# A transformer block on one core: the scores of its second attention as three products of high and low parts

## The chip, the core and the metric

The kernel runs on one core of a Trainium2 chip. The core has a matrix engine (TensorE, PE in the profile; its weight loads are PEld), a vector engine (VectorE, DVE), a scalar engine (ScalarE, ACT), a GpSimd engine (POOL) and a queue that starts transfers (SP). Each engine works through its own list of instructions in the order in which they stand there; an instruction waits at the head of its list until the semaphores that it names are set. TensorE adds up in PSUM; the other engines copy from there to SBUF. The metric is the device time of one execution in microseconds (us), and lower is better.

## The reference

Two layers of a block with three branches on 256 tokens `x` and 256 context tokens `ctx`, model width 1024, all in float32. In each layer the normed input goes through one wide projection; from it come a neighbourhood attention (the first attention here), a gated spatial mix, and the attention of this case, an ordinary softmax attention with 8 heads whose queries and keys are 96 wide:

```
s = einsum('bhqd,bhkd->bhqk', q_blk, k) * scale     # 96 wide
p = softmax(s);  out = einsum('bhqk,bhkd->bhqd', p, v)
y = g0 * (y_na @ na_w_o) + g1 * (y_gm @ gm_w_o) + g2 * (y_mla @ mla_w_o)
```

Queries of `x` see 512 keys (context and `x`), queries of the context see its own 256 keys, and the last layer has no queries of the context. The outputs of the three branches are gated, projected and added, and a squared-ReLU MLP follows.

## The kernel before, in words

All activations lie transposed, a feature per partition, and the 512 tokens (256 in what the last layer needs) are the moving columns of the matmuls. Nearly every product is made as three matmuls of high and low parts: a float32 tensor A is split into H, its value rounded to the type `fp32r` (a copy on ACT), and L = A - H (a subtraction on DVE), and the product is H·H + H·L + L·H in one PSUM sum (`mm3`, lines 276 to 278). Weights are loaded by SP and split on the way in (`split1`, lines 115 and 116). The scores of the second attention are the exception: `mla_score` (line 406) multiplies the plain float32 tensors `kml` and `qml` of a head, one matmul for a score tile of 128 queries by 512 or 256 keys.

The stage around the change, in each layer:

- `head_T` (lines 764 to 776) transposes the heads of keys and queries into PSUM (`h_tr`) and scales them into one tile a head: ACT the first 256 columns (line 771), DVE the other 256 where there are four token tiles (line 773).
- `soft_pv` (from line 416) runs four times, once for each pair of heads. For each of its score tiles: the scores `S` (PSUM, two buffers), the negative maximum `nm` on DVE, the exponential `P` on ACT with its sum, the reciprocal `r` and the scaling on DVE, the transposes `pt` on TensorE (PSUM, one buffer), and the copy `PT` of them on ACT. When a pair of heads is through, the products with the values follow (`pvm`), and `split_out` makes the high and low parts `yml` of the pair's output. A pair has four score tiles of 512 keys, and in layer 0 four of 256 keys besides.
- Between these steps TensorE works on the gates (`gate`) and the projections (`z`) of another branch (`merge`, one call of which stands after the attention in the text). `paced` and `tc.issue_after` tie each of their steps to a score matmul, so that these products are spread over the attention as filling work.

The order of the lists is made by a scheduler when the program is built: it takes instructions by priority, as their inputs and buffers come free in its own model of time. Most tiles that outlive a step share one pool of 34 buffers of 128x512 (`g2`, tag `g`): keys, queries, branch outputs, `yml`, and in the second layer the running `x`. A pair of 256-column parts shares one buffer (`parts`).

Of the kernel before, what the change touches and what calls it, by code (L numbers as in the profile page):

```python
# [9 lines left out]
AF = mybir.ActivationFunctionType  # L10
ALU = mybir.AluOpType
# [5 lines left out]
NX = 256  # L17
# [9 lines left out]
def hybrid_block_kernel(tc, a, out):  # L27
    nc = tc.nc
    act = nc.scalar.activation
    vec = nc.vector  # L30
    mm = nc.tensor.matmul

    from contextlib import ExitStack, nullcontext
    with ExitStack() as es:
# [12 lines left out]
        def psum(tag, name):  # L47
            return pp.tile([128, 512], F32, tag=tag, name=name, bufs={"mm": 4, "s": 2, "pt": 1, "pv": 1}[tag])


        def g2(name, dt=F32R):
            return gp.tile([128, 512], dt, tag="g", name=name, bufs=34)

        def views(name, T):

            while True:
                t = g2(name)
                if T == NX:
                    yield t[:, 0:NX]
                    yield t[:, NX:]  # L60
                else:
                    yield t

        def parts(name, T):

            v = views(name, T)
            return next(v), next(v)
# [333 lines left out]

            return score

        def mla_score(K, Q, h):
            def score(s, q0, k0, nk):
                return mm(s, lhsT=Q[h][0:96, q0:q0 + 128], rhs=K[h][0:96, k0:k0 + nk], start=True, stop=True)  # L406

            return score

        def split_out(ps, name, T):  # L410
            H, Lo = parts(name, T)
            act(out=H[:, :T], in_=ps[:, :T], func=AF.Copy)
            vec.tensor_tensor(out=Lo[:, :T], in0=ps[:, :T], in1=H[:, :T], op=ALU.subtract)
            return H, Lo

        def soft_pv(score, V, pv, streams, bias, marks):

            for v in range(streams):
                kts = [0, 1, 2, 3] if v == 0 else [2, 3]
                k0, nk = kts[0] * 128, 128 * len(kts)  # L420
                PT = [gp.tile([128, 4, NX], F32, tag="PT", name="PT", bufs=2) for _ in range(2)]
                for qt in range(2):
                    q0 = v * NX + qt * 128
                    S = []
                    for hh in range(2):
                        s = psum("s", "S")
                        marks.append(score[hh](s[:, :nk], q0, k0, nk).ins)
                        S.append(s)
                    for hh in range(2):
                        s = S[hh]  # L430
                        if bias is not None and v == 0:
                            vec.tensor_tensor(out=s[:, :NX], in0=s[:, :NX], in1=bias[hh][:, qt, :], op=ALU.add)
                        nm = sp.tile([128, 1], F32, tag="nm", name="nm")
                        vec.tensor_reduce(out=nm, in_=s[:, :nk], axis=AX.X, op=ALU.max, negate=True)
                        P = gp.tile([128, 512], F32, tag="P", name="P", bufs=2)
                        sm = sp.tile([128, 1], F32, tag="sm", name="sm")
                        act(out=P[:, :nk], in_=s[:, :nk], func=AF.Exp, bias=nm, accum_out=sm)
                        r = sp.tile([128, 1], F32, tag="r", name="r")
                        vec.reciprocal(r, sm)
                        vec.tensor_scalar(out=P[:, :nk], in0=P[:, :nk], scalar1=r, scalar2=None, op0=ALU.mult)  # L440
                        pt = psum("pt", "pt")
                        for i in range(len(kts)):
                            nc.tensor.transpose(pt[:, i * 128:(i + 1) * 128], P[:, i * 128:(i + 1) * 128], ident)  # L443
                        n = len(kts)
                        turned = act(out=PT[hh][:, :n, qt * 128:(qt + 1) * 128],
                                     in_=pt[:, :nk].rearrange("p (i q) -> p i q", i=n), func=AF.Copy)
                for i, kt in enumerate(kts):
                    for hh in range(2):
                        m = mm(pv[64 * hh:64 * hh + 64, v * NX:(v + 1) * NX], lhsT=V[kt][hh], rhs=PT[hh][:, i, :],
                               start=(i == 0), stop=(i == len(kts) - 1), tile_position=(0, 64 * hh))  # L450
                        if i == 0 and hh == 0:

                            tc.add_manual_dep(m.ins, turned.ins.name, mybir.DependencyInfo(
                                mybir.DependencyClass.Sync, mybir.DependencyReason.DATA), reason="both heads")
# [68 lines left out]
        for l in range(L):  # L523
            last = l == L - 1
# [21 lines left out]
            with tc.issue_after(last_load[0]):  # L546
                if l == 0:
# [8 lines left out]
                                  in_=a["kqrow"][l:l + 1, :].to_broadcast([128, 64]))  # L556
# [4 lines left out]
            for g in range(4):  # L561
                vec.scalar_tensor_tensor(out=bs[:, g, :], in0=rsum[:, g * 128:(g + 1) * 128],
                                         scalar=col[:, 28 + g:29 + g], in1=bs[:, g, :], op0=ALU.mult, op1=ALU.add)
# [74 lines left out]
            for t in range(4):  # L638
                vec.tensor_scalar(out=cnat[t][:, 0:128], in0=cnat[t][:, 0:128], scalar1=rsc[:, t:t + 1], scalar2=None,
                                  op0=ALU.mult)  # L640
# [42 lines left out]
            for t in tts:  # L683
                v = vn[t][:, :512]
                vec.tensor_scalar(out=v, in0=v, scalar1=mv[:, t, 0:1], scalar2=rv[:, t:t + 1], op0=ALU.subtract,
                                  op1=ALU.mult)
# [10 lines left out]
            for g in range(4):  # L697
                ps = psum("s", "sg")
                for t in tts:
                    mm(ps[:, t * 128:(t + 1) * 128], lhsT=vn[t][:, g * 128:(g + 1) * 128], rhs=wsT[:, g, :], start=True,  # L700
                       stop=True)
                y = tmp2("yg")
                for t in tts:
                    vec.scalar_tensor_tensor(out=y[:, t * 128:(t + 1) * 128], in0=ps[:, t * 128:(t + 1) * 128],
                                             scalar=col[:, 24 + g:25 + g], in1=bs[:, g, :], op0=ALU.mult, op1=ALU.add)
                vec.tensor_tensor(out=y[:, :T], in0=y[:, :T], in1=u[g][:, :T], op=ALU.mult)
                H, Lo = parts("yg", T)
# [8 lines left out]
            for j in range(4):  # L716
# [10 lines left out]
                H, Lo = split_out(pv, "yna", T)  # L727
# [10 lines left out]
            for t in range(4):  # L738
# [4 lines left out]
                for hf in range(2):  # L743
                    ps = psum("mm", "kv")
# [3 lines left out]
                        func=AF.Copy)  # L748
# [6 lines left out]
                                  op1=ALU.mult)  # L755
# [4 lines left out]
                                  in1=rb.to_broadcast([128, 8, 32]), op=ALU.mult)  # L760
# [3 lines left out]
            def head_T(tiles, colx, colc, name, n):  # L764
                res = []
                for h in range(8):
                    ps = psum("s", "h_tr")
                    for t in range(n):
                        nc.tensor.transpose(ps[0:96, t * 128:(t + 1) * 128], tiles[t][:, h * 96:(h + 1) * 96], ident)
                    o = g2(name, F32)  # L770
                    act(out=o[0:96, 0:256], in_=ps[0:96, 0:256], func=AF.Copy, scale=colx[0:96])
                    if n > 2:
                        vec.tensor_scalar(out=o[0:96, 256:512], in0=ps[0:96, 256:512], scalar1=colc[0:96], scalar2=None,
                                          op0=ALU.mult)
                    res.append(o)
                return res

            merge(l, 0, ygH, ygL, hH, hL, ymix, T, range(4, 6))
            kmT = head_T(knat, gq[:, 3:4], col[:, 6:7], "kml", 4)

            uq = [split(load(a["uq"][l, k], 768), 384) for k in range(2)]
            qnat = []
            for t in tts:
                ts = slice(t * 128, (t + 1) * 128)
                qn = nat("qnat")
                for hf in range(2):
                    ps = psum("mm", "qm")
# [21 lines left out]
                qnat.append(qn)  # L809
            merge(l, 0, ygH, ygL, hH, hL, ymix, T, range(6, 8))  # L810
            qmT = head_T(qnat, gq[:, 2:3], gq[:, 1:2], "qml", 2 * ns)


            ymH, ymL = [], []
            marks = []
            for j in range(4):
                pv = psum("pv", "pvm")
                soft_pv([mla_score(kmT, qmT, 2 * j + hh) for hh in range(2)],
                        [[vml[t][:, (2 * j + hh) * 64:(2 * j + hh + 1) * 64] for hh in range(2)] for t in range(4)],
                        pv, ns, None, marks)  # L820
                H, Lo = split_out(pv, "yml", T)
                ymH.append(H)
                ymL.append(Lo)
# [35 lines left out]
            if last:  # L859
# [3 lines left out]
                for n in range(KC):  # L863
                    H, Lo = h2[0][n], h2[1][n]
# [3 lines left out]
            for n in range(both, 8):  # L868
                out_chunk(a["wa"][l, 28 + n], n, mixH, mixL, [0], 16, acc)
                if last:  # L870
                    H, Lo = h2[0][n], h2[1][n]
                    act(out=H[:, :NX], in_=xT[n][:, :NX], func=AF.Copy, scale=aa2[:, n:n + 1])
                    vec.scalar_tensor_tensor(out=Lo[:, :NX], in0=xT[n][:, :NX], scalar=aa2[:, n:n + 1], in1=H[:, :NX],
                                             op0=ALU.mult, op1=ALU.subtract)
# [165 lines left out]
```

## Time and profile before

| what | value |
|---|---|
| median of 3 runs | 1408.24 us (1403.92 to 1413.73) |
| profiled execution, its own time | 1407.51 us |
| its span (first to last instruction) | 1405.5 us |
| mean granted TensorE clock | 0.998 |
| TensorE busy | 1372.3 us, 98% of the span |
| VectorE, ScalarE busy | 957.5 us (68%), 703.7 us (50%) |

The profile is of one execution. The busy time of TensorE counts each matmul from its start to the modelled end of its pipeline, so that matmuls that follow each other overlap; how long TensorE is kept by one is read from the start of one to the start of the next. A float32 matmul shows as two records, an `fp32r` matmul as one. The second attention runs from about 331 to 420 us in layer 0 and from about 1107 to 1160 us in layer 1.

### The profile page before, as it was taken

To read this page: it belongs to the slowest core of one execution; us is meant where nothing else is said; L and a number is where in the kernel's file an instruction comes from. 1 tells how busy PE (TensorE), PEld (TensorE's weight loads), DVE (VectorE), ACT (ScalarE), POOL (GpSimd) and SP (SyncE) were. 2 spreads that over 40 slices of the span, in tenths; PEclk is the share of its full clock that TensorE was granted. 3 is DMA by queue.
4 is the path that set the end of the run, shared out by engine and by line. 5 is a ranking of instruction groups with operands and counts; after the bars stand their busy time and mean duration, and the time that the engine had idled before them with its cause. 6 is when DMAs were issued, how large, how long until landed. Compare 5 with 4: busy or idle time off the path is not lost.

```text
span 1405.5 us, 22569 instructions
## 1 busy us (share of the span) xinstructions
PE 1372.3 (98%) x8438; PEld 1160.2 (83%) x8438; DVE 957.5 (68%) x2075; ACT 703.7 (50%) x1440; POOL 58.4 (4%) x35
## 2 busy tenths in 40 slices
PE   5999999999999999999999999999999999999999
PEld 3888767777667789987788888988878879999998
DVE  5666477664563458998766665787777766777775
ACT  4466256543453346623324234566666665656654
POOL 0110000110000000000000000011003000000000
PEclk9999999999999999999999999999999999999999
DMA  9423542234313465665555553442533425655564
GB/s 326 158 80 105 190 140 91 82 95 131 106 52 119 135 191 170 202 201 171 198 198 180 192 183 91 150 137 94 180 106 110 126 80 163 191 179 178 184 182 148
DMA packets 67213, 210.61 MB, mean 150 GB/s; under 512 B 8608, under 2 KB 9632, under 8 KB 67104
## 3 DMA queue, kind: packets, MB, share of 16 engines
q1 hardware_dynamic: 67104, 209.18, 46.2%
q8 instruction: 66, 1.08, 0.3%
q14 instruction: 43, 0.35, 0.1%
HBM read 208.10 MB, written 1.05 MB: 149 GB/s over the span
## 4 chain that ended last, share of the span: by engine, by line
PE 94%; DVE 2%; DMA 2%; ACT 1%; issue 0%; SPq 0%; POOL 0%; ACTq 0%; DVEq 0%
PE o_ps L277 8%; PE o_ps L278 8%; PE o_ps L276 8%; PE f L276 6%; PE f L277 6%; PE f L278 6%; PE gate L276 5%; PE gate L278 5%; PE gate L277 5%; PE b_ps L276 4%; PE b_ps L278 4%; PE b_ps L277 4%; PE pt L443 3%; PE S L406 2%; PE z L276 2%; PE z L277 2%
## 5 line engine op out<-in xcount | busy, mean ns | idle before, releaser
L115 ACT ACTIVATE wh<-raw 128x512 fp32r<-128x512 f32 (+2 forms) x570 | 352.8, 626 | 522.9 <-PE o_ps L277 188.5
L116 DVE TENSOR_TENSOR wl<-raw,wh 128x512 fp32r<-128x512 f32 (+2 forms) x570 | 384.8, 682 | 184.3 <-ACT wh L115 179.6
L276 PE MATMUL f<-hH,wh 128*128 128x258 f32 (+2 forms) x560 | 180.7, 324 | 0.5 <-ACT wh L115 0.5
L278 PE MATMUL f<-hH,wl 128*128 128x258 f32 (+2 forms) x560 | 180.7, 323 | 0.1
L277 PE MATMUL f<-hL,wh 128*128 128x258 f32 (+2 forms) x560 | 180.6, 324 | 0.2 <-DVE hL L266 0.2
L277 PE MATMUL o_ps<-aL,wh 128*128 128x256 f32 (+1 forms) x544 | 176.3, 327 | 1.6 <-DVE aL L909 1.6
L276 PE MATMUL o_ps<-aH,wh 128*128 128x256 f32 (+1 forms) x544 | 175.8, 328 | 0.0
L278 PE MATMUL o_ps<-aH,wl 128*128 128x256 f32 (+1 forms) x544 | 175.5, 327 | 0.0
L276 PE MATMUL gate<-hH,wh 128*128 128x512 f32 (+1 forms) x384 | 140.4, 366 | 0.0
L278 PE MATMUL gate<-hH,wl 128*128 128x512 f32 (+1 forms) x384 | 130.9, 341 | 0.0
L277 PE MATMUL gate<-hL,wh 128*128 128x512 f32 (+1 forms) x384 | 130.4, 340 | 0.0
L276 PEld LDWEIGHTS f<-hH,wh 128*128 128x128 f32 x560 | 105.9, 190 | 10.2 <-ACT wh L115 2.0
L278 PEld LDWEIGHTS f<-hH,wl 128*128 128x128 f32 x560 | 106.1, 190 | 8.5 <-DVE wl L116 0.3
L277 PEld LDWEIGHTS f<-hL,wh 128*128 128x128 f32 x560 | 105.9, 190 | 8.7 <-issue 0.4
L277 PEld LDWEIGHTS o_ps<-aL,wh 128*128 128x128 f32 x544 | 103.0, 190 | 10.6 <-DVE aL L909 2.1
L276 PEld LDWEIGHTS o_ps<-aH,wh 128*128 128x128 f32 x544 | 102.5, 190 | 10.1 <-ACT wh L115 1.2
L278 PEld LDWEIGHTS o_ps<-aH,wl 128*128 128x128 f32 x544 | 102.7, 190 | 8.8
L277 PE MATMUL b_ps<-wl,hH 128*128 128x512 f32 (+2 forms) x288 | 108.3, 379 | 0.0
L278 PE MATMUL b_ps<-wh,hL 128*128 128x512 f32 (+2 forms) x288 | 106.2, 380 | 0.0
L197 DVE SCALAR_TENSOR_TENSOR macc<-rawx,sS,macc 128x512 f32<-128x512 f32 x112 | 78.9, 748 | 39.8 <-DMA rawx<-in_wmod_dram 39.7
L276 PE MATMUL b_ps<-wh,hH 128*128 128x512 f32 (+2 forms) x288 | 103.1, 384 | 0.2 <-ACT hH L265 0.2
L276 PEld LDWEIGHTS gate<-hH,wh 128*128 128x128 f32 x384 | 73.0, 190 | 15.8 <-issue 7.5
(226 smaller groups left out, 2481.6 us busy)
## 6 DMA issues: line engine op xcount, KB each, us to landing
raw<-in_wa_dram SPq DMA_DIRECT2D x147, 512.0 KB, 3.6
raw<-in_w_dram SPq DMA_DIRECT2D x68, 512.0 KB, 3.6
raw<-in_wb_dram SPq DMA_DIRECT2D x32, 512.0 KB, 3.3
raw<-in_wmod_dram SPq DMA_DIRECT2D x32, 512.0 KB, 3.4
rawx<-in_wmod_dram SPq DMA_DIRECT2D x32, 512.0 KB, 4.6
raw<-in_wo_dram SPq DMA_DIRECT2D x24, 512.0 KB, 3.6
rawm<-in_wmod_dram SPq DMA_DIRECT2D x32, 256.0 KB, 6.0
rawx<-in_wmod_dram SPq DMA_DIRECT2D x32, 256.0 KB, 4.3
```

What stands on the lines that cost most here:

```text
L115: act(out=wh[:, :width], in_=src, func=AF.Copy)
L116: vec.tensor_tensor(out=wl[:, :width], in0=src, in1=wh[:, :width], op=ALU.subtract)
L197: vec.scalar_tensor_tensor(out=o, in0=src, scalar=s, in1=o, op0=ALU.mult, op1=ALU.add)
L276: mm(ps, lhsT=sh, rhs=mh, start=first, stop=False)
L277: mm(ps, lhsT=sh, rhs=ml, start=False, stop=False)
L278: mm(ps, lhsT=sl, rhs=mh, start=False, stop=last)
L406: return mm(s, lhsT=Q[h][0:96, q0:q0 + 128], rhs=K[h][0:96, k0:k0 + nk], start=True, stop=True)
L443: nc.tensor.transpose(pt[:, i * 128:(i + 1) * 128], P[:, i * 128:(i + 1) * 128], ident)
```

## The change: three products for each score, and parts made pair by pair

```diff
-        def mla_score(K, Q, h):
+        def mla_score(K, Q):
+            (KH, KL), (QH, QL) = K, Q
             def score(s, q0, k0, nk):
-                return mm(s, lhsT=Q[h][0:96, q0:q0 + 128], rhs=K[h][0:96, k0:k0 + nk], start=True, stop=True)
+                qs, ks = slice(q0, q0 + 128), slice(k0, k0 + nk)
+                mm(s, lhsT=QH[0:96, qs], rhs=KH[0:96, ks], start=True, stop=False)
+                mm(s, lhsT=QH[0:96, qs], rhs=KL[0:96, ks], start=False, stop=False)
+                return mm(s, lhsT=QL[0:96, qs], rhs=KH[0:96, ks], start=False, stop=True)
             return score
+        def split_head(t):
+            H, Lo = g2("hdH"), g2("hdL")
+            act(out=H[0:96, :], in_=t[0:96, :], func=AF.Copy)
+            vec.tensor_tensor(out=Lo[0:96, :], in0=t[0:96, :], in1=H[0:96, :], op=ALU.subtract)
+            return H, Lo
...
+                    if n == 2:
+                        H, Lo = parts(name, NX)
+                        act(out=H[0:96, :], in_=ps[0:96, 0:NX], func=AF.Copy, scale=colx[0:96])
+                        vec.scalar_tensor_tensor(out=Lo[0:96, :], in0=ps[0:96, 0:NX], scalar=colx[0:96], in1=H[0:96, :],
+                                                 op0=ALU.mult, op1=ALU.subtract)
+                        res.append((H, Lo))
+                        continue
...
-                soft_pv([mla_score(kmT, qmT, 2 * j + hh) for hh in range(2)],
+                heads = [[split_head(kmT[h]), qmT[h] if last else split_head(qmT[h])] for h in (2 * j, 2 * j + 1)]
+                soft_pv([mla_score(*z) for z in heads],
```

Each score becomes three `fp32r` matmuls. The keys of all heads, and the queries in layer 0, are still made as float32 tiles by `head_T`; just before a pair's `soft_pv` `split_head` makes `hdH` (ACT) and `hdL` (DVE), 96x512, for its two heads. In layer 1 the queries (256 columns) are split as they leave PSUM.

The change moves instructions at the seam from one pair of heads to the next. On TensorE in layer 0, from the last score tile of the second pair to the first of the third (`S` are scores, `pt` the transposes, `pvm` the products with the values, `gate` the filling work), before:

```order
L449 MATMUL pvm<-PT,vml 64x256 x8
L443 MATMUL pt<-ident,P 128x128 x2
L406 MATMUL S<-kml,qml 128x256
L276 MATMUL gate<-hH,wh 128x512
L277 MATMUL gate<-hL,wh 128x512
L278 MATMUL gate<-hH,wl 128x512
L443 MATMUL pt<-ident,P 128x128 x2
L406 MATMUL S<-kml,qml 128x512
L276 MATMUL gate<-hH,wh 128x512
L277 MATMUL gate<-hL,wh 128x512
L278 MATMUL gate<-hH,wl 128x512
```

and the same place after the change:

```order
L411 MATMUL S<-hdL,hdH 128x256
L412 MATMUL S<-hdH,hdL 128x256
L276 MATMUL gate<-hH,wh 128x512
L277 MATMUL gate<-hL,wh 128x512
L278 MATMUL gate<-hH,wl 128x512
L455 MATMUL pt<-ident,P 128x128 x6
L461 MATMUL pvm<-PT,vml 64x256 x4
L410 MATMUL S<-hdH 128x512
L411 MATMUL S<-hdL,hdH 128x512
L412 MATMUL S<-hdH,hdL 128x512
L276 MATMUL gate<-hH,wh 128x512
```

Before, the first score of the next pair stood between two transposes of the old pair, with filling work around it; now all transposes and value products of the old pair stand in a row, and the next pair's scores behind them. The other two seams of layer 0 read alike (the first has four `mod_ps` matmuls of 256 columns more ahead of the transposes).

On ACT at the same seam after the change (`yml` is the output of the old pair, `hdH` the high parts of the next):

```order
L457 ACTIVATE PT<-pt 128x2x128 x2
L424 ACTIVATE yml<-pvm 128x512
L418 ACTIVATE hdH<-kml 96x512
L418 ACTIVATE hdH<-qml 96x512
L418 ACTIVATE hdH<-kml 96x512
L418 ACTIVATE hdH<-qml 96x512
L449 ACTIVATE P,sm<-S,nm 128x512
```

The four high parts stand behind `yml`, and `yml` waits for `pvm`; DVE has the same order (the low part of `yml`, four `hdL`, then `nm`). In layer 1 the seams read so on TensorE after the change, three times:

```order
L276 MATMUL gate<-hH,wh 128x256
L277 MATMUL gate<-hL,wh 128x256
L278 MATMUL gate<-hH,wl 128x256
L455 MATMUL pt<-ident,P 128x128 x12
L461 MATMUL pvm<-PT,vml 64x256 x8
L410 MATMUL S<-hdH,qml 128x512 x2
L411 MATMUL S<-hdL,qml 128x512
L412 MATMUL S<-hdH,qml 128x512
L276 MATMUL gate<-hH,wh 128x256
```

(at the third seam with `z` in place of `gate`). Before, each group of four transposes there was followed by a score of the next pair and about twelve filling matmuls.

## Rows read from the trace of the kernel before

**Rows 1.** The page, busy time, share of the span and instructions of each engine.

```profile
PE 1372.3 (98%) x8438; PEld 1160.2 (83%) x8438; DVE 957.5 (68%) x2075; ACT 703.7 (50%) x1440; POOL 58.4 (4%) x35
```

**Rows 2.** Stretches of both second attentions: length, busy PE, PEld, DVE, ACT, POOL, clock, DMA.

```profile
330.00:420.00 90.00, 90.00 (x472) 62.60 (x471) 51.95 (x119) 45.75 (x112) 0.00 (x0) 1.00 0.28 88
1107.00:1160.00 53.00, 52.80 (x360) 42.01 (x360) 35.32 (x78) 32.73 (x74) 0.00 (x0) 1.00 0.27 85
```

**Rows 3.** Groups by shape on PE: records, busy us, mean ns; idle before.

```profile
L406 PE MATMUL S<-kml,qml 96*128 96x512 f32 x64 | 32.7, 594 | 0.2 <-ACT qml L771 0.2
...
L406 PE MATMUL S<-kml,qml 96*128 96x256 f32 x32 | 9.7, 383 | 0.0
```

**Rows 4.** Timeline of PE, layer 0, two 512-key scores: start, us, instruction.

```profile
330.98 1.88 PE L406 MATMUL S<-kml,qml 96*128 96x512 f32 x4
332.30 0.80 PE L278 MATMUL gate<-hH,wl 128*128 128x512 f32 x1
332.94 0.40 PE L276 MATMUL gate<-hH,wh 128*128 128x512 f32 x1
```

**Rows 5.** Timeline of PE, layer 0, one 256-key score.

```profile
353.61 0.60 PE L406 MATMUL S<-kml,qml 96*128 96x256 f32 x2
...
354.28 0.39 PE L277 MATMUL gate<-hL,wh 128*128 128x512 f32 x1
```

**Rows 6.** Timeline of PE, first attention of layer 1: two fp32r products and gates.

```profile
1013.43 0.40 PE L399 MATMUL S<-naK,naQ 128*128 128x512 f32 x1
...
1013.90 0.28 PE L276 MATMUL gate<-hH,wh 128*128 128x256 f32 x1
1014.01 0.27 PE L277 MATMUL gate<-hL,wh 128*128 128x256 f32 x1
```

**Rows 7.** Groups by shape on ACT and DVE that split high and low parts.

```profile
L115 ACT ACTIVATE wh<-raw 128x512 fp32r<-128x512 f32 x546 | 340.1, 630 | 502.1 <-PE o_ps L277 188.5 <-PE f L277 118.6 <-DMA raw<-in_wa_dram 72.4
...
L116 DVE TENSOR_TENSOR wl<-raw,wh 128x512 fp32r<-128x512 f32 x546 | 371.3, 687 | 178.1 <-ACT wh L115 173.7 <-PE pt L443 0.2
...
L390 DVE SCALAR_TENSOR_TENSOR naQL<-tr_ps,gq,naQ 64x256 fp32r<-64x256 f32 x16 | 7.7, 483 | 2.3 <-ACT naQ L388 2.0
```

**Rows 8.** Timelines of PE, ACT and DVE, layer 0, around a seam.

```profile
357.38 0.44 PE L443 MATMUL pt<-ident,P 128*128 128x128 f32 x2
357.92 0.39 ACT L445 ACTIVATE PT<-pt 128x256 f32<-128x256 f32 x1 [0.46 <-PE pt L443]
...
367.02 1.08 PE L449 MATMUL pvm<-PT,vml 128*64 128x256 f32 x8
368.15 0.60 ACT L412 ACTIVATE yml<-pvm 128x512 fp32r<-128x512 f32 x1 [0.82 <-PE pvm L449]
368.78 0.69 DVE L413 TENSOR_TENSOR yml<-pvm,yml 128x512 fp32r<-128x512 f32 x1 [1.16 <-ACT yml L412]
```

**Rows 9.** Timelines of layer 1: transposes in a row, and a pair's value products.

```profile
1058.63 0.63 PE L443 MATMUL pt<-ident,P 128*128 128x128 f32 x4 [0.19 <-DVE P L440]
...
1059.30 0.60 ACT L445 ACTIVATE PT<-pt 128x512 f32<-128x512 f32 x1 [0.83 <-PE pt L443]
1059.95 0.66 PE L443 MATMUL pt<-ident,P 128*128 128x128 f32 x4 [0.69 <-ACT PT L445]
...
1151.01 1.95 PE L449 MATMUL pvm<-PT,vml 128*64 128x256 f32 x16
...
1153.00 0.39 ACT L412 ACTIVATE yml<-pvm 128x256 fp32r<-128x256 f32 x1 [2.13 <-PE pvm L449]
```

**Rows 10.** Timeline of PE, layer 1, the first scores of the second attention.

```profile
1106.49 0.79 PE L769 MATMUL h_tr<-ident,qnat 128*96 128x128 f32 x4 [0.20 <-ACT qml L771]
1107.47 1.13 PE L406 MATMUL S<-kml,qml 96*128 96x512 f32 x2 [0.20 <-ACT qml L771]
```

**Rows 11.** Stretches of layer 1, first attention; columns as in rows 2.

```profile
1015.00:1018.40 3.40, 1.84 (x11) 1.21 (x10) 2.33 (x7) 2.73 (x6) 0.00 (x0) 1.00 0.54 154
1018.40:1022.00 3.60, 3.58 (x16) 3.39 (x16) 3.17 (x9) 1.78 (x4) 0.00 (x0) 0.53 0.13 35
1057.00:1061.30 4.30, 2.30 (x13) 1.33 (x13) 2.13 (x7) 2.66 (x6) 0.00 (x0) 1.00 0.30 95
```

## The prediction

> **What bounds the kernel now.** I read the page first: TensorE is busy 98% of the span [rows 1], so a microsecond taken from its list, or put on it, moves the end one for one, and work of another engine counts only where TensorE waits for it. Then the stretches of the changed stage [rows 2]: in layer 0 TensorE is busy all 90 of 90 us, in layer 1 for 52.8 of 53, at the full clock, while VectorE has 58 to 67% and ScalarE 51 to 62%. So there is room beside TensorE for more work of those two, and no slack on TensorE. Last the timelines, for what one score costs TensorE and for how long the steps of a softmax follow each other [rows 4 to 6, 8, 9]. The profiled execution took 1407.51 us, 2.0 more than its span and 0.7 less than the median of the runs; the sums below stand on it.
>
> **The change part by part.**
>
> *Scores.* There are 32 score tiles of 512 keys and 16 of 256: 64 and 32 records [rows 3], two for each. Two 512-key scores start at 330.98, one gate matmul follows, the next begins at 332.94 [rows 4]; less 0.23 for that gate, 1.73 us for two, 0.865 each. For 256 keys: 0.67 us from 353.61 to 354.28 with one gate between, so 0.44 [rows 5]. An `fp32r` product of 512 columns keeps TensorE for 0.235 us (two from 1013.43 to 1013.90), one of 256 for about 0.115 [rows 6]. Three of them are 0.70 and 0.35. Saved: 32 x 0.165 + 16 x 0.09 = **6.7 us**. Those products have 128 rows and the new ones 96; I take no difference for that, and rival 4 is the far end of it.
>
> *Parts.* 24 `hdH` at 0.63 us on ScalarE and 24 `hdL` at 0.69 on VectorE [rows 7], 15.1 and 16.5 us, and 8 new subtractions of 0.48 for the queries of layer 1 (row L390 is the nearest, out of PSUM, 256 columns). Against the idle time of both engines [rows 2] this is covered in the middle of a pair. What it costs if the cover is gone is the next two terms: where TensorE has nothing else in front of it.
>
> *The seams of layer 0, three.* After the change the six transposes, four value products and the first scores of the next pair stand in a row on TensorE, with no filling work between, and TensorE cannot go past a waiting one. I count from the start of the transposes. There is one `pt` buffer, so each of the three pairs of transposes waits until ScalarE has copied the one before: 0.54 us from `pt` to `PT` and 0.39 of copying [rows 8], with the hand-over 0.97, three times 2.9. From `pvm` to ScalarE's `yml` 1.13, from there to VectorE's `yml` 0.63 [rows 8]. The parts of the next pair stand behind these in both lists: on VectorE the rest of `yml`, `hdL` of the keys and `hdL` of the queries, three of 0.69, until the third product can start, and 0.23 for it. Sum 7.0 us. Of this TensorE works 0.8 (transposes, 0.44 each less the 0.17 by which a record is longer than its step), 0.9 (value products) and 0.7 (three products): 2.4. Lost **4.6 us**, three times 13.7.
>
> *The seams of layer 1, three.* Twelve transposes, eight value products, then scores. A turn of four transposes takes 1.32 us where they stand in a row [rows 9], three 4.0. From `pvm` to `yml` 1.99 [rows 9], 0.39 for it, 0.63 for `hdH`, 0.69 for `hdL`, 0.47 for the last two products: 8.1 us. TensorE works 1.4, 1.8 and 0.9 (four products) in it. Lost **4.0 us**, three times 12.0.
>
> *The start of layer 1.* Transposed queries leave PSUM through two buffers. Now each is free only after VectorE's subtraction behind ScalarE's copy: 0.48 and a hand-over of 0.05 more in each of the last three rounds, 1.6. Before, the first score came 0.98 us after the last transposes began [rows 10]; now `hdH` and `hdL` (0.63 + 0.69) stand between, of which two products fill 0.4: 0.9. Together **2.5 us**. In layer 0, 22 matmuls of 512 columns (`z` and `gate`) stand in TensorE's list between the last transposed queries and the first score, 22 x 0.235 = 5.2 us, and VectorE's four parts take 4 x 0.69 = 2.8: nothing.
>
> *The clock.* In the first attention of layer 1 TensorE was busy 1.84 of 3.4 us, with a wait of over a microsecond at the end, and the granted clock then stood at 0.53 for 3.6 us (half speed, 1.2 GHz, for nearly all of it) while TensorE was fully busy; the loss is 3.6 x 0.47 = 1.7 us [rows 11]. Further on it was busy 2.30 of 4.3 us, in a row of transposes as at the seams, and kept the full 2.4 GHz. So the trace has it both ways. At a seam of layer 0 TensorE works 2.4 of 7.0 us, with some 3 us in front of the last two products that hold one product; that is sparser than the stretch that fell, and I take a fall there, 3 x 1.7 = **5.1 us**. A seam of layer 1 works 4.1 of 8.1, more than the stretch that held; I take none. The Trainium skill (TensorE: Matmul & The Clock Gate, HAM oscillation) says that a TensorE left waiting between bursts is throttled to half rate and pays in the next burst, each time anew. By the rule alone every seam and the start would pay, 11.9 us in place of 5.1; rows 11 agree once and disagree once.
>
> Sum: 1407.5 - 6.7 + 13.7 + 12.0 + 2.5 + 5.1 = **1434 us**.
>
> *Bounds.* A seam cannot cost less than the turns alone, if the parts were ready when the value products end: two waits for `PT` between transposes and one before `pvm`, 0.69 each in layer 1 [rows 9] (the second wait stands in its row), about as much in layer 0: 2.1 us. With the start and no fall that gives 1407.5 - 6.7 + 12.6 + 2.5 = 1416. Upward, one exponential (some 0.7 us) or one weight split (0.63 and 0.69) may stand in front of a copy at each seam: six times 0.7, 4 us, on top of the case with every fall.
>
> **The rivals.**
>
> 1. *The clock falls everywhere* (the rule above, Trainium skill): six seams and the start at 1.7 us. 1407.5 - 6.7 + 28.2 + 11.9 = 1441. For it: the wait of half a microsecond or more before the scores at every seam. Against it: the stretch that held.
> 2. *The seams cost only their turns*, 1416, within the measurement's noise of 1% about 1408. For it: `hdH` waits for nothing but its place behind `yml`, and VectorE and ScalarE may have run ahead. Against it: `yml` itself waits for `pvm`, and both lists have the parts behind it.
> 3. *Not slower: the seams cost nothing*, because the old pair's `P` and `PT` are there long before TensorE comes to them, as before, where in 330 to 420 us it never waited [rows 2]. Then the cheaper scores are left: 1407.5 - 6.7 + 2.5 = 1403. It decides at (6.7 - 2.5) / 6 = 0.7 us lost per seam: under that the change is faster. Against it: one `PT` turn alone is 0.97 us with 0.27 of work in it.
> 4. *The scores do not get cheaper*: if each product took the two records of a float32 one, 32 x 1.73 + 16 x 0.88 = 69 us more. The first attention multiplies the same type at one record, so I give it under 1%.
>
> **How the numbers follow.** Chances: the forecast 0.60, rival 1 0.20, rival 2 0.14, rival 3 0.05, rival 4 under 0.01. Predicted 1434. The range leaves out rival 3, most of what lies under the bound of rival 2 and the far end of rival 1: 1416 to 1446; the forecast's own range is 1426 to 1441. A change under 1%, 14 us, cannot be told from none by a few runs of this kernel. Slower by over 1% (from 1422 up) are the forecast and rival 1: 0.81; within 1% are rivals 2 and 3 but for a sliver: 0.17; faster by over 1% would need 14 us, twice all that the scores can save: 0.02.
>
> **What would show it.** In the new profile: scores at one record each, three per tile, about 0.235 us from start to start at 512 keys; at six places a row of `pt`, `pvm`, `S` without filling work, 7 to 8 us long, in which TensorE waits for `PT`, then for `hdH` and `hdL`, 4 to 5 us a place; waits for the queries' VectorE subtraction before the first scores of layer 1; the granted clock at half after the seams of layer 0 and full after those of layer 1. Outside the two stages the lists are the same, so all of the difference must lie in them. It would be wrong if TensorE shows no waits at the seams (rival 3), if it waits for `PT` but not for the parts (rival 2), or if the clock falls after all seams or none.

## The result and the profile after

The changed kernel takes 1439.66 us (median of 4 runs, 1436.75 to 1442.93) where the kernel before took 1410.01 on the same chip: a ratio of 1.0224, 95% interval 1.0202 to 1.0246. Forecast were 1434 us and a range of 1416 to 1446. The profiled execution took 1440.59 us with a span of 1438.6, 33.1 longer than that of before.

The page's busy line of the changed kernel, to be read against [rows 1]:

```profile
PE 1384.7 (96%) x8486; PEld 1174.5 (82%) x8486; DVE 977.3 (68%) x2107; ACT 716.9 (50%) x1464; POOL 59.3 (4%) x35
```

VectorE and ScalarE got 20 and 13 us of work more, which is what the parts cost there, and their share did not rise. TensorE fell from 98 to 96%. Its busy time rose by 12 us although the scores are cheaper: time at half clock counts as busy. So both losses have to be looked for on TensorE, waiting and clock. Its waits in the changed kernel (what waited, for whom: us in total, times, longest):

```profile
PE S L410 <- ACT hdH L418: 9.2, 7, 1.7
PE pt L455 <- ACT PT L457: 6.6, 10, 0.7
PE pt L455 <- DVE P L452: 5.4, 8, 0.9
PE pvm L461 <- ACT PT L457: 3.5, 6, 0.7
PE h_tr L781 <- DVE qml L785: 2.6, 2, 2.0
```

Seven waits of scores for the parts are the six seams and the start of layer 1; six waits of `pvm` for `PT` are the six seams again. One seam of layer 0, as the timeline of three engines shows it (start, us, instruction, idle time before it and who ended that):

```profile
361.70 0.44 PE L455 MATMUL pt<-ident,P 128*128 128x128 f32 x2
362.24 0.38 ACT L457 ACTIVATE PT<-pt 128x256 f32<-128x256 f32 x1 [1.16 <-PE pt L455]
...
362.67 0.44 PE L455 MATMUL pt<-ident,P 128*128 128x128 f32 x2 [0.53 <-ACT PT L457]
...
363.88 0.41 PE L455 MATMUL pt<-ident,P 128*128 128x128 f32 x2 [0.77 <-DVE P L452]
...
364.76 1.40 PE L461 MATMUL pvm<-PT,vml 128*64 128x256 f32 x8 [0.47 <-ACT PT L457]
366.20 0.60 ACT L424 ACTIVATE yml<-pvm 128x512 fp32r<-128x512 f32 x1 [1.50 <-PE pvm L461]
366.69 0.62 ACT L418 ACTIVATE hdH<-kml 96x512 fp32r<-96x512 f32 x1
366.83 0.69 DVE L425 TENSOR_TENSOR yml<-pvm,yml 128x512 fp32r<-128x512 f32 x1 [3.10 <-ACT yml L424]
...
367.44 0.68 DVE L419 TENSOR_TENSOR hdL<-kml,hdH 96x512 fp32r<-96x512 f32 x1
...
367.88 0.79 PE L410 MATMUL S<-hdH 96*128 96x512 f32 x1 [1.72 <-ACT hdH L418]
368.04 0.68 DVE L419 TENSOR_TENSOR hdL<-qml,hdH 96x512 fp32r<-96x512 f32 x1
...
368.90 0.67 PE L412 MATMUL S<-hdH,hdL 96*128 96x512 f32 x1
...
369.37 0.63 PE L276 MATMUL gate<-hH,wh 128*128 128x512 f32 x1
```

Read it down: TensorE turns `pt` and waits for its copy; then `pvm`; then ScalarE's `yml`, which needs `pvm`, and only behind it the first `hdH` of the next pair; on VectorE the same with `hdL`. ScalarE was idle for 1.50 us and VectorE for 3.10 in front of `yml`: they had time for the parts, and the parts stood in the wrong place. The row is 7.67 us from the first `pt` to the first `gate` (forecast 7.0), and the gate matmuls behind it take 0.63 instead of 0.40: the clock is at half.

A score of 512 keys after the change, at full clock, on TensorE's timeline, where [rows 4] show two records of a float32 score:

```profile
374.14 0.40 PE L410 MATMUL S<-hdH 96*128 96x512 f32 x1
374.37 0.40 PE L411 MATMUL S<-hdL,hdH 96*128 96x512 f32 x1
374.60 0.39 PE L412 MATMUL S<-hdH,hdL 96*128 96x512 f32 x1
374.83 0.39 PE L276 MATMUL gate<-hH,wh 128*128 128x512 f32 x1
```

Three products from 374.14 to 374.83 are 0.69 us for 0.865, as in the sum.

What each place cost can be read from stretches of 16 us around the seven rows: three seams of layer 0, the start of layer 1, its three seams (columns as in [rows 2]: length, busy PE, ..., granted clock).

```profile
361.00:377.00 16.00, 12.51 (x56) 8.53 (x56) 8.67 (x18) 7.65 (x19) 0.00 (x0) 0.79 0.22 66
387.00:403.00 16.00, 12.50 (x56) 8.53 (x53) 7.72 (x18) 7.79 (x19) 0.00 (x0) 0.79 0.11 34
416.00:432.00 16.00, 12.51 (x52) 9.01 (x51) 9.17 (x21) 7.28 (x19) 0.00 (x0) 0.79 0.06 22
1115.00:1131.00 16.00, 12.28 (x73) 10.11 (x73) 11.20 (x24) 8.31 (x19) 0.00 (x0) 0.79 0.34 109
1134.00:1150.00 16.00, 12.72 (x81) 9.71 (x80) 8.27 (x18) 7.97 (x18) 0.00 (x0) 0.89 0.12 33
1150.00:1166.00 16.00, 12.65 (x90) 10.35 (x89) 9.61 (x22) 8.96 (x21) 0.00 (x0) 1.00 0.30 92
1168.00:1184.00 16.00, 12.65 (x78) 9.42 (x77) 8.12 (x18) 7.94 (x19) 0.00 (x0) 0.89 0.20 66
```

The loss of a stretch is its idle time plus busy time x (1 - clock). A seam of layer 0: 3.49 + 12.51 x 0.21 = 6.1, three 18.4. The start of layer 1: 3.72 + 2.58 = 6.3, of which 0.9 was idle in the kernel before as well (1097 to 1170 us: 72.08 busy of 73). Its seams: 4.7, 3.4 and 4.7, together 12.8. So 18.4 + 5.4 + 12.8 = 36.6, less 6.7 for the scores is 29.9. The stretches are from the two profiled executions, and these differ by 33.1, so 3.2 us lie in no stretch, and what they are is not shown. That the medians differ by 29.65, close to the 29.9, is luck: the profile of before lies 2.5 under its median, that of the change 0.9 above.

A second way to cut the time, used for the experiments: the stage of layer 0 from the first transpose of its queries to the first output product (`o_ps` from `mix`), and that of layer 1 from the start of the last `z` of its gated branch to the start of the last such output product. Each kernel's times are from its own profiled execution, the ratio is to the kernel before on the same chip.

| kernel | layer 0, us | layer 1, us | ratio (95%) |
|---|---|---|---|
| before | 192.8 | 126.9 | 1 |
| the change | 208.3 | 144.7 | 1.0224 (1.0202 to 1.0246) |
| bare products, no parts | 188.9 | 124.2 | 0.9942 (0.9925 to 0.9959) |
| layer 0 alone changed | 208.6 | 128.4 | 1.0117 (1.0097 to 1.0137) |
| layer 1 alone changed | 192.8 | 143.8 | 1.0128 (1.0108 to 1.0149) |
| parts a pair ahead | 189.9 | 131.7 | 1.0016 (1.0002 to 1.0029) |
| only more buffers | 197.4 | 136.4 | 1.0078 (1.0055 to 1.0101) |
| parts made, not read | 194.3 | 134.5 | 1.0061 (1.0038 to 1.0083) |
| ahead, queries copied | 189.8 | 129.3 | 0.9987 (0.9974 to 0.9999) |
| seams filled | 205.1 | 144.6 | 1.0205 (1.0177 to 1.0233) |
| ahead, first pair float32 | 189.8 | 126.9 | 0.9949 (0.9932 to 0.9966) |
| the change, queries copied | 208.6 | 144.2 | 1.0219 (1.0193 to 1.0244) |

### The profile page after: what moved, and what is told of

Read it like the earlier page. It is cut to its first block, busy times and chain, and to the rows that moved or that the text cites. A ratio compares the mean times of both kernels' runs of the same rounds, so it can differ in the third digit from the quotient of the medians.

```text
span 1438.6 us, 22735 instructions
## 1 busy us (share of the span) xinstructions
PE 1384.7 (96%) x8486; PEld 1174.5 (82%) x8486; DVE 977.3 (68%) x2107; ACT 716.9 (50%) x1464; POOL 59.3 (4%) x35
## 5 line engine op out<-in xcount | busy, mean ns | idle before, releaser
L115 ACT ACTIVATE wh<-raw 128x512 fp32r<-128x512 f32 (+2 forms) x570 | 352.9, 626 | 526.5 <-PE o_ps L277 189.8
L276 PE MATMUL gate<-hH,wh 128*128 128x512 f32 (+1 forms) x384 | 132.5, 345 | 0.0
L859 DVE SCALAR_TENSOR_TENSOR xT<-o_ps,modT,xT 128x256 f32<-128x256 f32 x120 | 54.7, 481 | 44.0 <-PE o_ps L278 43.6
```

Of the source, the lines that this page charges most:

```text
L115: act(out=wh[:, :width], in_=src, func=AF.Copy)
L276: mm(ps, lhsT=sh, rhs=mh, start=first, stop=False)
L859: vec.scalar_tensor_tensor(out=xT[n][:, s], in0=ps[:, p0:p0 + NX], scalar=modT[:, v, mod0 + n:mod0 + n + 1], in1=xT[n][:, s], op0=ALU.mult ...
```

## The experiments

**1. Bare products.**

```
-                    if n == 2:
+                    if False:
...
-                    o = g2(name, F32)
+                    o = g2(name)
...
-                heads = [[split_head(kmT[h]), ...] for h in (2 * j, 2 * j + 1)]
+                heads = [[(kmT[h], kmT[h]), (qmT[h], qmT[h])] for h in (2 * j, 2 * j + 1)]
```

> Three fp32r products per score, no parts: keys and queries are written once as fp32r, the same high part stands in for the low parts (the low parts are left out of the computation). Theory (the scores themselves are cheaper, the seams cost): TensorE keeps its filling work between the transposes and the products at all six seams, no waits for parts, 32 x 0.165 + 16 x 0.09 = 6.7 us less than before, some 1403. Rival (three products are not cheaper than one float32 product): within 2 us of before, or slower.

Measured 1397.45 us against 1405.87, 8.4 less. In the stages the scores bring 3.9 in layer 0 and 2.7 in layer 1: 6.6, where the forecast had 6.7. The rest lies outside the two stages. A part of it can be the half-clock stretch of [rows 11], worth 1.7: the granted clock of this profiled execution is 1.000 over the whole of it. For the medians this is not shown. Between 330 and 430 us TensorE never waits:

```profile
330.00:430.00 100.00, 100.00 (x583) 74.71 (x582) 57.99 (x132) 49.20 (x122) 0.00 (x0) 1.00 0.29 93
```

The saving is real and as large as forecast, and three products in place of one disturb nothing: no wait and no fall of the clock came with them here. What the change loses comes from getting the parts to them: against this kernel it loses 19.4 us in layer 0 (forecast 13.7 + 5.1 = 18.8) and 20.5 in layer 1 (forecast 12.0 + 2.5 = 14.5).

**2 and 3. One layer alone.** In the other layer, the scores stay one float32 product (`mla_score1` is the `mla_score` of before). The edit for layer 0 alone; layer 1 alone has the two cases the other way round:

```
+  heads = [[kmT[h], qmT[h]] for h in ...] if last else [[split_head(kmT[h]), split_head(qmT[h])] for h in ...]
...
+  soft_pv([(mla_score1 if last else mla_score)(*z) for z in heads], ...)
...
-                    if n == 2:
+                    if False:
```

> The change in layer 0 alone, layer 1 as before. By the trace of the changed kernel the stage of layer 0 grew by 15.5 us (forecast 14.7): 1425. If the change of layer 0 also moves the clock of what follows, the time comes out beside this by the 1.7 us of each fall more or less. Rival (the cost goes by the amount of added work on ScalarE and VectorE, evenly): half of 30, 1425 as well, but then without waits of TensorE at the three seams.

> The change in layer 1 alone, layer 0 as before. By the trace of the changed kernel the stage of layer 1 grew by 17.8 us: 1428. By the forecast's terms (4.0 a seam, 2.5 for the start, no fall of the clock) 11.9: 1422. If the clock at the seams falls by chance of phase, other seams than the first and third should show it now, since everything arrives at another time.

Measured 1422.32 and 1424.58 against 1405.87: 16.5 and 18.7. The stages grew by 15.8 and 16.9 where in the whole change they grew by 15.5 and 17.8, so in the stages the two layers' costs add up (the medians' 16.5 and 18.7 add to 35.2, beside 29.65 in the whole change and 33.1 between its profiled executions; the intervals of the ratios leave room for that). With layer 0 alone changed, scores wait three times for `hdH`, 5.2 us in all, which its rival excluded. Layer 1 alone lies between the 1422 of the forecast's terms and the 1428 by the trace. Two sizes are worth a look. With layer 0 alone changed, the untouched layer 1 is 1.5 longer than before: its start, which waited 0.9 us before and held the full clock, waits 1.1 and has a fall of the clock (granted 0.89 over 1116 to 1132 us). And with layer 1 alone changed, the clock did not fall at other seams than in the whole change, which I had expected from chance: the value products show it, 3.35 us long at the first seam, 1.95 at the second, 3.57 at the third.

**4. Parts a pair ahead.** The parts of the next pair are asked for in front of a pair's softmax, in eight more buffers under two tags (`nat`, `bias`) that are idle in this stage.

```
+            heads = pair_heads(0)
             for j in range(4):
                 pv = psum("pv", "pvm")
-                heads = [[split_head(kmT[h]), ...] for h in (2 * j, 2 * j + 1)]
+                nxt = pair_heads(j + 1) if j < 3 else None
                 soft_pv(...)
+                heads = nxt
```

Here `pair_heads(j)` makes the parts of pair `j` by the `split_head` of the change, in the buffers that `head_room` of experiment 5 hands out.

> All the changed arithmetic, but the parts of a pair of heads are made a pair ahead, into eight more buffers (two tags that are idle in this stage). TensorE's list has its filling work at all six seams again. Theory (the seams are the price): six seams and their falls of the clock go, the cheaper scores stay, and the start of layer 1 with its slow release of two PSUM buffers stays at 2.5 to 6: 1406 to 1410, against 1440 of the change. Rival (the price is the parts' work, 24 x 0.63 on ScalarE and 24 x 0.69 on VectorE, crowding the softmax): no more than a few us better than the change, 1430 to 1440, with TensorE waiting for P and PT all over the stages.

Measured 1408.06 us, ratio 1.0016, as the theory had it: the same arithmetic, the same parts, and some 30 us less than the change. TensorE's list has its filling work at all six seams, and neither a wait nor a fall is left there; the start of layer 1 is left (stretches as above):

```profile
330.00:430.00 100.00, 100.00 (x574) 74.33 (x570) 64.03 (x144) 53.61 (x130) 0.00 (x0) 1.00 0.28 90
1094.00:1118.00 24.00, 20.06 (x119) 17.08 (x118) 18.30 (x39) 13.50 (x31) 0.00 (x0) 0.79 0.33 108
1118.00:1170.00 52.00, 52.00 (x405) 46.79 (x403) 34.46 (x75) 32.05 (x71) 0.00 (x0) 1.00 0.29 92
```

VectorE is busy for 64% of those 100 us and ScalarE for 54%, where they had 58 and 51 before [rows 2], and TensorE never waits for them. The stage of layer 1 is 7.5 us above that of the bare products, nearly all of it in the start: 3.9 idle, 1.1 of which the bare products have too, and 20.06 x 0.21 = 4.2 by the clock. The 7.5 are three times the 2.5 that the forecast gave the start.

**5. Only more buffers.** The same eight buffers, but each pair's parts are asked for where the change has them, behind the pair before.

```
+  room = head_room(4 if last else 8)      # so many of tag "g", then 6 of "nat" and 2 of "bias", in turn
...
-            H, Lo = g2("hdH"), g2("hdL")
+            H, Lo = next(room), next(room)
```

> The change with eight more buffers for the parts and nothing else altered: the program still makes the parts of a pair after the pair before. TensorE's list then keeps its filling work at four of the six seams; the second seam of layer 0 and the third of layer 1 stay a row of pt, pvm, S. Theory (too few buffers put the parts behind yml, and each row costs): one row of layer 0 (5.2) and one of layer 1 (4 to 6) above the kernel with parts made a pair ahead, 1417 to 1420 at 1406 of before. Rival (the price is the parts' work or the program's order of parts and pairs): near the change, 1435.

Measured 1416.76 against 1406.78, a ratio of 1.0078. Four of the six seams close by the buffers alone: with more room the scheduler puts those parts forward by itself. The two that stay open (the second of layer 0, the third of layer 1) are rows of `pt`, `pvm` and `S` as in the change. The one of layer 0:

```profile
381.59 0.44 PE L464 MATMUL pt<-ident,P 128*128 128x128 f32 x2 [1.02 <-ACT PT L466]
...
382.79 0.41 PE L464 MATMUL pt<-ident,P 128*128 128x128 f32 x2 [0.76 <-DVE P L461]
...
383.67 1.08 PE L470 MATMUL pvm<-PT,vml 128*64 128x256 f32 x8 [0.47 <-ACT PT L466]
...
386.49 0.79 PE L410 MATMUL S<-hdg 96*128 96x512 f32 x1 [1.73 <-ACT hdg L427]
```

They cost 7.5 and 4.7 us of their stages against the kernel of experiment 4. So at four seams it was the pool of 34 buffers that put the parts behind `yml`: with eight more they moved. The other two close only where the parts are also asked for a pair ahead (experiment 4). Asking a pair ahead without the eight buffers was not run.

**6. Parts made, but not read.** `split_head` runs as in the change, and the scores are one float32 product of `kmT` and `qmT` (the queries of layer 1 are copied as before besides).

```
                 heads = [[split_head(kmT[h]), ...] for h in (2 * j, 2 * j + 1)]
+                heads = [[kmT[h], qmT[h]] for h in (2 * j, 2 * j + 1)]
...
-                soft_pv([mla_score(*z) for z in heads],
+                soft_pv([mla_score1(*z) for z in heads],
```

> All parts made as in the change (and the queries of layer 1 also copied as before), but the scores are one float32 product of keys and queries as before, so nobody reads the parts. Theory (waiting for the parts is the price, making them is not): no waits for hdH or PT at the seams, within 5 us of before, 1406 to 1411. Rival (the work on ScalarE and VectorE is the price): 1420 to 1435.

Measured 1414.76 against 1406.78, 8.0 more: more than the theory's 5, less than the rival's 13 and above, so neither range holds it. The stretches tell where (columns as above):

```profile
330.00:430.00 100.00, 99.31 (x523) 68.85 (x522) 60.69 (x140) 53.74 (x132) 0.00 (x0) 1.00 0.27 90
1096.00:1122.00 26.00, 20.68 (x125) 16.42 (x124) 17.64 (x40) 15.71 (x37) 0.00 (x0) 0.80 0.35 117
1122.00:1180.00 58.00, 57.87 (x418) 47.64 (x417) 39.16 (x86) 37.26 (x83) 0.00 (x0) 1.00 0.27 82
```

Away from the start TensorE waits 0.7 us in layer 0, whose whole stage is 1.5 longer than before, and 0.1 in layer 1; at the start of layer 1 the parts' work comes with 5.3 us of idle time and 4.1 by the clock. There TensorE has few other products left and its transposes wait for ScalarE's copies (4.6 us of waits of `h_tr` for `qml`), and here work put between those copies showed.

**7. The start, mended in part.** As 4, but the queries of layer 1 leave PSUM by one copy of ScalarE, as before, and are split from SBUF (into the same eight buffers and, in layer 1, eight of tag `g` in place of four).

```
-                    if n == 2:
+                    if False:
...
-  qmT[h] if last else split_head(qmT[h], room)
+  split_head(qmT[h], room, T)
```

> Parts made a pair ahead, and the queries of layer 1 leave PSUM as before, by one copy of ScalarE, and are split from there like the keys. Theory: the waits for the VectorE subtraction of the queries (2.6), the wait of the first score (1.4) and the half clock from 1104 to 1114 (5 us) that the kernel with parts a pair ahead shows at the start of layer 1 all go: 9 less, some 1398 to 1400, faster than before by 6 to 8. Rival (those waits only move to the new splits behind the copies): 1403 to 1408.

Measured 1404.60 against 1406.78, ratio 0.9987 (0.9974 to 0.9999): inside the rival's range, though a part of the theory holds. The start, and the first score in it:

```profile
1094.00:1118.00 24.00, 21.09 (x143) 18.72 (x142) 18.76 (x40) 15.41 (x38) 0.00 (x0) 0.93 0.36 116
```

```profile
1105.61 0.50 PE L410 MATMUL S<-hdg 96*128 96x512 f32 x1 [1.90 <-ACT hdg L427]
```

The waits for VectorE's subtraction are gone, and the start loses 2.9 us of idle time and 1.5 by the clock, where experiment 4 had 3.9 and 4.2. But the first score waits 1.9 us for its `hdH` (here `hdg`), where it waited 1.4: ScalarE had parts of the second pair and the last copies in front of the first pair's.

**8. Filled seams.** The change, with work of no use for TensorE in the three rows of layer 0.

```
+                            for _ in range(3 - hh):
+                                mm(pt[:, 384:512], lhsT=P[:, 0:128], rhs=ident, ...)
...
+                    f = psum("pt", "fill")
+                    for _ in range(7):
+                        mm(f[:, 0:128], lhsT=PT[1][:, 0, 0:128], rhs=ident, ...)   # behind pvm
```

> The change with 12 small products of no use at each seam of layer 0, put where TensorE waits: behind the last two groups of transposes (3 and 2) and between pvm and S (7), each about 0.22 us long at full clock, into columns and a buffer that nobody reads. Theory (the clock falls because TensorE idles in the row, and costs 1.7 a seam; the row's length is set by ScalarE and VectorE): full clock in the three rows, no longer rows, 5 us less than the change, ratio to before 1.019 in place of 1.022 to 1.024. Rival (the fall does not hang on idling, or the half-clock stretch costs nothing since TensorE waits there anyway): no gain, or up to 3 us longer.

Measured 1433.57 against 1406.78, ratio 1.0205 (1.0177 to 1.0233); by the runs alone that can't be told from the change's 1.0224. The trace shows the mechanism. First the stretch over all three rows, then the first row on TensorE:

```profile
356.00:440.00 84.00, 79.23 (x475) 60.04 (x474) 47.07 (x106) 43.48 (x107) 0.00 (x0) 1.00 0.20 63
```

```profile
357.77 0.44 PE L455 MATMUL pt<-ident,P 128*128 128x128 f32 x2
...
359.01 0.83 PE L458 MATMUL pt<-ident,P 128*128 128x128 f32 x6
360.32 0.44 PE L455 MATMUL pt<-ident,P 128*128 128x128 f32 x2 [0.47 <-ACT PT L460]
360.60 0.61 PE L458 MATMUL pt<-ident,P 128*128 128x128 f32 x4
361.68 1.08 PE L464 MATMUL pvm<-PT,vml 128*64 128x256 f32 x8 [0.47 <-ACT PT L460]
362.69 1.83 PE L473 MATMUL fill<-ident,PT 128*128 128x128 f32 x14
364.50 0.50 PE L410 MATMUL S<-hdH 96*128 96x512 f32 x1
...
365.72 0.40 PE L276 MATMUL gate<-hH,wh 128*128 128x512 f32 x1
```

With products of no use in the gaps the granted clock is 1.00 through all three rows, where it was 0.79 in each, and the gates behind the row take 0.40 instead of 0.63. Chance is no likely reason: in experiments 2 and 10, whose layer 0 is that of the change, the clock fell at each of these rows too (granted 0.79, 0.89, 0.79 and 0.89, 0.79, 0.79 over 16 us), nine falls of nine without such products and none of three with them. (That `pvm` takes 1.08 here and 1.40 in the change says little: it takes 1.08 at all three rows of experiments 2 and 10 as well, where the fall comes behind it.) The stage gets 3.2 us shorter. It is not 5 because the fillers stand in the way: `pvm` starts 3.9 us after the first `pt`, where it was 3.1 in the change, an estimated 2.5 us over the three rows. So at these rows it is idling that makes the clock fall, and taking the three falls away gave back 3.2 us, an estimated 5.7 with that delay added; counted as busy time x (1 - clock) they were 7.9.

**9. First pair in float32.** As 7, and the first pair of layer 1 keeps the products of before, so that nothing waits for its parts.

```
+  heads = [[kmT[h], qmT[h]] for h in range(2)] if last else pair_heads(0)
...
+  (mla_score1 if last and j == 0 else mla_score)(*z)
```

> Parts a pair ahead, queries of layer 1 copied and split from the copy, and the first pair of layer 1 keeps its float32 products, so the first scores of that layer wait for no parts. Theory (what is left above the kernel of bare products is the start of layer 1): the wait of 1.9 and the half clock from 1104 to 1112 go, four scores cost 0.165 more each: stage of layer 1 some 125 to 126 us against 129.3 with split first pair, 126.9 before and 124.2 for bare products; 1401 to 1403 at 1407 of before, ratio 0.996 to 0.997. Rival (the copies and parts of the start stay in the way of the transposes): no better than 0.9987.

Measured 1401.37 against 1407.21, ratio 0.9949 (0.9932 to 0.9966): half a percent faster than the kernel before, and a ratio of 1 lies outside the interval. At the start of layer 1, 1.3 us of idle time and a short fall are left:

```profile
1094.00:1118.00 24.00, 22.73 (x150) 18.99 (x149) 19.63 (x46) 16.61 (x39) 0.00 (x0) 0.93 0.40 127
```

The time came out as expected, the stage of layer 1 a little longer (126.9 for 125 to 126) and no shorter than before. The 3.0 us that its profiled execution, the slowest of nine, saves in the two stages are all in layer 0; the other 2.8 between the medians are in no stage and stay unexplained.

**10. The change, queries copied.** The edit of 7 on the change itself, without more buffers:

```
-                    if n == 2:
+                    if False:
...
-  qmT[h] if last else split_head(qmT[h])
+  split_head(qmT[h], T)
```

> The change, but the queries of layer 1 leave PSUM by one copy as before and are split per pair like the keys. The seams of layer 1 then carry four parts of the queries more (0.42 each on both engines). Theory (the start is worth some 5 to 7 us of the layer's 17.8, the seams 12 to 13): the waits of the transposes for the VectorE subtraction (2.6) go, the wait of the first score stays, 2 to 3 us less at the start, and each seam gets up to 0.8 longer by the second subtraction: within 3 us of the change, ratio 1.021 to 1.024. Rival (the start is no more than the 2.5 forecast and the seams are the undersized term): 1.5 less at the start at the most and 2 to 3 more at the seams, 1.024 to 1.026.

Measured 1439.40 against 1407.21, ratio 1.0219. The waits for VectorE's subtraction went (2.6 us), and waits of scores for `hdH` grew from 9.2 to 10.5. It is inside the theory's range, but the two theories' numbers lie too close together for this run to tell them apart; experiment 4 does that.

## Why the prediction was right, point by point

- *Scores, 6.7 us saved.* Right: 6.6 in the stages (experiment 1).
- *Parts, hidden in the middle of a pair.* Right: with the parts made a pair ahead TensorE is busy for 100 of 100 us in layer 0 with all of them in the lists, and the stage is 1.0 longer than with bare products (experiment 4). Making them for nobody brings 0.8 us of waits outside the start of layer 1 (experiment 6).
- *Seams of layer 0, 4.6 lost and 1.7 by the clock each.* Right in sum, 6.1 for 6.3, with another split: 3.5 of idle time (4 to 5 were to be seen) and 2.6 by the clock. Part of the row itself, `pvm` and the products, runs at half clock, and so is busy where the forecast had it idle. The third `pt` waits for `P`, 0.77 us, because its exponential stands between the copies on ScalarE; the forecast had an exponential in front of a copy in its upper bound.
- *Seams of layer 1, 4.0 each.* Near in sum by luck, 12.8 for 12.0: the idle time is less than forecast, 3.3 each, and the clock, for which I had nothing, makes up for it. I had none there because a row of transposes had held the full clock [rows 11]. It fell at two of three seams, 1.4 each; the value products of the three show it:

```profile
1140.71 3.37 PE L461 MATMUL pvm<-PT,vml 128*64 128x256 f32 x16 [0.69 <-ACT PT L457]
...
1158.26 1.95 PE L461 MATMUL pvm<-PT,vml 128*64 128x256 f32 x16 [0.69 <-ACT PT L457]
...
1174.41 3.58 PE L461 MATMUL pvm<-PT,vml 128*64 128x256 f32 x16 [0.69 <-ACT PT L457]
```

- *Start of layer 1, 2.5 us.* Mis-sized, and the largest error of a term: 5.4 in the change, 7.5 in experiment 4. The waits are those named (2.6 for the subtraction, 1.1 for the parts; less the 0.9 of before 2.8, for 2.5). Missing was the fall of the clock behind them, 2.6, which the forecast left out without a reason of its own. The gates behind the first scores show it, 0.41 us where 256 columns take 0.28 at full clock [rows 6]:

```profile
1122.44 0.81 PE L781 MATMUL h_tr<-ident,qnat 128*96 128x128 f32 x4 [1.96 <-DVE qml L785]
1123.94 1.09 PE L781 MATMUL h_tr<-ident,qnat 128*96 128x128 f32 x4 [0.69 <-DVE qml L785]
1126.11 1.31 PE L410 MATMUL S<-hdH,qml 96*128 96x512 f32 x2 [1.08 <-ACT hdH L418]
...
1128.07 0.41 PE L276 MATMUL gate<-hH,wh 128*128 128x256 f32 x1
```

- *The clock.* Three falls in layer 0, as forecast; in layer 1 three of four places fell where none had been forecast, so the sign "full after those of layer 1" failed at two of three seams. The reason given for it does not hold: 4.1 of 8.1 us is 51%, not more than the 53% of the stretch that held (2.30 of 4.3), and the stretch that fell was the busier of the two (1.84 of 3.4, 54%). The two stretches of [rows 11] could not decide it. Rival 1 had all seven places fall. Six of seven is nearer to it than to the forecast; in time the measured 29.65 more lies between the 26.5 of the forecast and the 33.4 of rival 1, and the 33.1 of the profiled executions at rival 1. The rule of the Trainium skill (TensorE: Matmul & The Clock Gate, HAM oscillation), read as rival 1 reads it, agrees with the trace at six of seven places; the section tells of longer waits, for transfers, so it is rival 1's reading that the agreement bears out. Experiment 8 shows for layer 0 that idling is the cause; for layer 1 that is argued from the likeness of the rows.
- *The total.* Set against bare products the stages lose 19.4 us in layer 0, where 18.8 was forecast, and 20.5 in layer 1, where it was 14.5. The range holds the time either way, but the medians, 3.4 us nearer to each other than the profiles, make the sum look better than its terms: layer 1 is 6.0 short, through the clock above all.
- *Rivals 2 and 3.* Refuted by the waits of scores for `hdH` at all six seams. Rival 4 by experiment 1.
- That the buffers decide the order of the lists was not in the forecast, which took the order as it stood. Experiment 5 shows it for four of six seams.

What stays open: which of the alike seams of layer 1 fall. The first and third did in the change and in experiments 3 and 8, though everything came 15 and 7 us earlier there. In experiment 10, whose start and seams differ, only the second did: its `pvm` took 1.95, 3.00 and 1.95 us. But that row is not quite like its neighbours: its third group of transposes waits 1.26 us for `P`, where the others wait 0.9.

## What to carry to other kernels

A step that is cheaper on the bound engine can lose many times its gain through where its inputs are made: look whether the next block's preparation stands behind the last block's result in the helpers' lists, and whether a full buffer pool put it there. The same work one block ahead, in buffers that happen to be idle, turned 2.2% slower into nearly no change (0.2% slower), and with the queries copied and the first block of layer 1 left as they were into 0.5% faster. Each wait of the bound engine should be priced with a half-clock stretch behind it, as a chance: one row of the same kind that held the full clock does not show that the next will.

## What the runs showed of the hardware

- A fall of the clock, counted as busy time x (1 - granted clock), came to 1.4 to 2.6 us a place, up to three quarters of the waiting beside it (2.6 beside 3.5 in layer 0). Taking three of them away gave back less than that count: 3.2 us for 7.9, with an estimated 2.5 lost to the products that did it (experiment 8).
- Work of no use kept the clock up: 3.3 us of it in a row of 8 us (0.83, 0.61 and 1.83) made the granted clock 1.00 for 0.79.
- Rows of the same instructions, with waits alike to 0.1 us and 16 to 18 us apart, fell or held in turn: half, full, half in three kernels (the change, experiments 3 and 8).
